# Two finest levels of the hgrn2 chunk matrix: products on VectorE and sums on GpSimd instead of 32-lane matmuls on TensorE

## The chip, the cores and the metric

The kernel runs on one core of a Trainium2 chip. The time is that of one execution of the whole program on the device, in microseconds (us). Five engines work side by side, each through its own instructions in a fixed order: TensorE (PE, matmuls; PEld, its weight loads), VectorE (DVE), ScalarE (ACT), GpSimd (POOL) and SyncE (SP, which issues the loads). They wait for each other on semaphores alone.

## The reference

Two layers work on 272 tokens (16 meta tokens and 256 others). Each layer has a mixer with three branches (retention, hgrn2, differential attention) and a convolutional feed-forward part. What the change touches is hgrn2, cut here to one chunk of 128 tokens:

```python
def step(state, xs):
    qc, kc, vc, lfc = xs                       # lfc: log of the forget gate
    cb = jnp.cumsum(lfc, axis=1)
    rel = cb[:, :, None] - cb[:, None, :]
    dec = jnp.where(causal, jnp.exp(jnp.where(causal, rel, 0.0)), 0.0)
    a = jnp.einsum('bqhd,bkhd,bqkhd->bhqk', qc, kc, dec)
    o = jnp.einsum('bhqk,bkhe->bqhe', a, vc) + jnp.einsum('bqhd,bhde->bqhe', qc * jnp.exp(cb), state)
    ...
```

The decay between a query and a key differs in each of the 128 features d, so `a` is no plain matmul. There are 8 heads of 128 features.

## The kernel before, in words

**The main stream.** Nearly all of the time goes to the dense products of the layers. Weights stand in memory as 128x128 tiles in the order of their use, eight to a chunk. A chunk is loaded (`wraw`), ScalarE makes a rounded copy (`whi`) and VectorE the rest (`wlo` = `wraw` - `whi`); three of `wraw` and four each of `whi` and `wlo` exist at a time. For each weight tile TensorE runs three matmuls over up to 272 tokens: `whi` by `xh`, `whi` by `xl`, `wlo` by `xh` (lines L900 to L902). Such a group is called a triple here. `_Weights.next` writes this.

**The order.** Nothing is issued as it is written. Every operation is recorded with an engine, an estimated cost and a due time, and `_Plan.order` sorts the whole program into one fixed order for each engine by a list schedule over these estimates. Line L592 is the recorder's, so nearly all operations but the matmuls of the main stream carry it. The main stream's place in time sets the due times of the rest (`behind`, `settle`): the work of hgrn2 is spread between triples. The estimate for a reduction over partitions is 0.4 us and 5.4 ns a column.

**hgrn2.** `hg_heads(b)` does four heads: it runs twice in a layer, so four times in the program. `k` is the tile `hf`, `q` the tile `hq`, both with features on partitions and 4 heads x 272 tokens along the free side. `total` holds the decay of each block of tokens, first the gate itself (`he`), then one level after the other in `tot`. A loop runs over the levels s = 1, 2, 4, 8, 16, 32, 64. On each level TensorE multiplies keys of left halves by queries of right halves of blocks of 2s tokens (a block of up to 32 small matmuls, tile `lev`, line L1084); VectorE puts the entries that belong to the level into `near` by a masked copy; then `q` and `k` are multiplied by `total` (two products), and the next level begins. So TensorE, in its fixed order, stands before each `lev` block until VectorE has done the two products of the level before. Level 1 also yields the diagonal. For level 2 a copy of queries (`extra`, by ScalarE) is used, and a second set of entries (right of each pair by itself) comes out of the same block. Where s is 32, `near` is copied to `at`, the matrix that `hg_outputs` multiplies by the values. The last 16 tokens go another way (`kt`, `qt`, `pm`, `am`) that the change leaves alone.

**GpSimd** normalises: `inverse` sums squares over the 128 partitions by `partition_all_reduce` (tile `hr`), for each head of each branch. It also clears tiles and copies small ones.

Of the kernel before, what the change touches and what calls it, by code (L numbers as in the profile page):

```python
# [15 lines left out]
AF = mybir.ActivationFunctionType  # L16
# [4 lines left out]
P = 128  # L21
# [3 lines left out]
T = META + SEQ  # L25
# [239 lines left out]
def _constants():  # L265
    f = np.float32
    c = np.zeros((P, C_END), f)
    c[:, C_COS_R : C_COS_R + T], c[:, C_SIN_R : C_SIN_R + T] = _rope_tables(RET_DK, 1)
    c[:, C_COS_D : C_COS_D + T], c[:, C_SIN_D : C_SIN_D + T] = _rope_tables(DA_DH, 2)
    k = np.arange(P)  # L270
    c[:, C_MASK + T - P : C_MASK + T] = np.where(k[None, :] <= k[:, None], 0.0, MASKED)
    c[:, C_IDENT : C_IDENT + P] = np.eye(P, dtype=f)
    lg = np.log1p(-np.exp2(-5.0 - np.arange(RET_HEADS, dtype=f))).astype(f)
    def decay(keys, queries):
        gap = (queries[None, :] - keys[:, None]).astype(f)
        d = np.exp(lg[None, :, None] * np.maximum(gap, 0)[:, None, :]) * f(RET_DK ** -0.5)
# [29 lines left out]
    block = [level(s, 32, 16) for s in LEVELS[2:6]] + [odd(32, 16), even(32, 32)]  # L306
    lev[:, :112] = np.tile(np.concatenate(block, axis=1), (4, 1))
# [344 lines left out]
def _trace(ctx, tc, plan, a, depth, probe):  # L652
# [26 lines left out]
    def slot(name, dt=F32):  # L679
        return new(sp, [P, 4 * T], dt, "slot", SLOTS, name)  # L680
# [13 lines left out]
    def bank(name):  # L694
        return new(bp, [P, 512], F32, "bank", 2, name)
# [4 lines left out]
    def tt(out, x, y, op):  # L700
        dve.tensor_tensor(out=out, in0=x, in1=y, op=op)
# [266 lines left out]
    for li in range(depth):  # L968
# [72 lines left out]
        def hg_heads(b):  # L1041
# [28 lines left out]
            def right(t, s):  # L1070
                return halves(t, s, t.shape[2])[:, :, :, 1, :]
# [22 lines left out]
            extra = slot("extra")  # L1094
# [3 lines left out]
            tt(right(q, 1), right(q, 1), right(total, 1), MUL)  # L1098
            room, at0 = slot("tot"), 0
            for i, s in reversed(list(enumerate(LEVELS))):  # L1100

                pl = bank("lev")
                wide = pl[:, :256].rearrange("p (g t) -> p g t", g=8)
                some = pl[:, :128].rearrange("p (g t) -> p g t", g=8)
                tokens = lambda c, t: slice(c * P + 32 * t, c * P + 32 * t + 32)
                if s == 1:
                    quarters(wide, q, lambda hd, c, t: q[:, hd, tokens(c, t)])
                    dve.copy_predicated(near, lev[:, 80:112].unsqueeze(1).to_broadcast([P, 8, 32]), wide)  # L1110
                elif s == 2:
                    act.activation(odd[:, :, :, :64].rearrange("p h c (n s) -> p h c n s", s=2),
                                   q[:, :, : 2 * P].rearrange("p h (c n two s) -> p h c n two s", c=2, two=2, s=2)[:, :, :, :, 1, :], AF.Copy)
                    quarters(wide.rearrange("p g (two t) -> p g two t", two=2), odd,
                             lambda hd, c, t: odd[:, hd, c, :].rearrange("p (two t) -> p two t", two=2)[:, :, 16 * t : 16 * t + 16])
                    fill(right(near, 2), lev[:, 48:64], wide[:, :, :16])
                    fill(right(near, 1), lev[:, 64:80], wide[:, :, 16:])
                elif s < 32:
                    quarters(some.rearrange("p g (n s) -> p g n s", s=s), q, lambda hd, c, t: right(q[:, hd : hd + 1, tokens(c, t)], s)[:, 0])
                    fill(right(near, s), lev[:, 16 * (i - 2) : 16 * (i - 1)], some)  # L1120
                elif s == 32:
                    for t in range(4):
                        here = slice(32 * t, 32 * t + 32)
                        act.activation(at[here, :, : 2 * P].rearrange("p h (c t) -> p h c t", c=2)[:, :, :, here],
                                       near[here].rearrange("p (h c) t -> p h c t", c=2), AF.Copy)

                    far = some.rearrange("p (h two) t -> p h (two t)", two=2)
                    blocks([(far[64 * n + 32 * c : 64 * n + 32 * c + 32, hd], k[:, hd, c * P + 64 * n : c * P + 64 * n + 32],
                             q[:, hd, c * P + 64 * n + 32 : c * P + 64 * n + 64]) for hd in hs for n in range(2) for c in range(2)], far, q)
                    for n in range(2):  # L1130
                        for c in range(2):
                            x = far[64 * n + 32 * c : 64 * n + 32 * c + 32]
                            to = at[64 * n : 64 * n + 32, :, c * P + 64 * n + 32 : c * P + 64 * n + 64]
                            if c:
                                act.activation(to, x, AF.Copy)
                            else:
                                dve.tensor_copy(to, x)
                else:

# [12 lines left out]
                    act.activation(at[:64, :, P + 64 : 2 * P], far[64:, :, :64], AF.Copy)  # L1152
                    act.activation(at[:, :, tail], far[:, :, 64:], AF.Copy)
# [450 lines left out]
```

## Time and profile before

| what | value |
|---|---|
| time, median of 3 runs | 1308.76 us (1308.33 to 1309.17) |
| the profiled execution's own time | 1309.57 us |
| its span in the trace | 1307.8 us |
| TensorE busy, matmuls | 1295.4 us (99%), 11774 matmuls |
| VectorE busy | 959.0 us (73%) |
| ScalarE busy | 801.6 us (61%) |
| GpSimd busy | 169.8 us (13%), 204 instructions |
| granted TensorE clock | 0.999 |

The span is the time from the first to the last instruction in the trace. Some 1.8 us of the profiled execution lie outside it, and that execution is 0.8 us above the median. An instruction's row in the timeline gives its start, its duration, engine, line, tiles (written <- read) and shape, and in brackets how long its engine had been idle and what ended that. Matmuls overlap each other, so the time that one costs TensorE is read from start to start.

### The profile page before, as it was taken

Reading aid. Unit: us, or ns where it says so; the run is one execution under the profiler, and the core shown is the slowest. Engines: PE = TensorE matmul, PEld = TensorE weight load, DVE = VectorE, ACT = ScalarE, POOL = GpSimd, SP = SyncE. Lnnn points to the kernel's source line nnn. Section 1 sums busy time; section 2 is a strip of 40 time slices with the busy share of each in tenths; the row PEclk is TensorE's granted clock in tenths of the full one; section 3 lists DMA queues with packets and bytes.
Section 4 is the critical chain, followed back from the end, with each engine's and each line's share of the span. In section 5 each row is a group of like instructions: output and inputs, shape, how many; then the busy total and the mean of one; then the engine's idle time right before and its main releaser. Section 6 shows DMA issues by size and latency. Waiting matters only on the chain.

```text
span 1307.8 us, 28691 instructions
## 1 busy us (share of the span) xinstructions
PE 1295.4 (99%) x11774; PEld 1266.6 (97%) x11774; DVE 959.0 (73%) x1589; ACT 801.6 (61%) x1332; POOL 169.8 (13%) x204
## 2 busy tenths in 40 slices
PE   9999999999999999999999999999999999999998
PEld 8999999999999999999999999999999999999986
DVE  7675787697576789886575757876986867888853
ACT  6747454746676577666456574547565775767643
POOL 5001101312222020000030011012131210200000
PEclk9999999999999999999999999999999999999999
DMA  7644543443544545555555445444445446466553
GB/s 268 202 143 160 168 160 134 146 146 129 193 131 162 179 160 176 182 175 181 177 177 186 162 152 177 150 144 146 156 147 176 142 165 202 144 199 205 200 188 112
DMA packets 60755, 219.06 MB, mean 168 GB/s; under 512 B 6864, under 2 KB 6992, under 8 KB 60624
## 3 DMA queue, kind: packets, MB, share of 16 engines
q1 hardware_dynamic: 60336, 216.71, 49.0%
q8 instruction: 92, 1.51, 0.5%
q10 hardware_dynamic: 288, 0.52, 0.1%
q14 instruction: 39, 0.32, 0.1%
HBM read 216.16 MB, written 1.05 MB: 166 GB/s over the span
## 4 chain that ended last, share of the span: by engine, by line
PE 92%; DVE 5%; ACT 1%; DMA 1%; issue 1%; SPq 0%; POOL 0%; DVEq 0%; ACTq 0%
PE main L900 27%; PE main L902 26%; PE main L901 26%; PE fo L1403 2%; PE fo L1404 2%; PE fo L1405 2%; DVE wlo L592 1%; PE lev L1084 1%; DVE two_b L592 1%; PE ds L1268 1%; PE ro L592 1%; PE ho L592 1%; PE vt L592 1%; DVE two_a L592 1%; PE do L592 1%
## 5 line engine op out<-in xcount | busy, mean ns | idle before, releaser
L900 PE MATMUL main<-xh,whi 128*128 128x272 f32 (+1 forms) x2368 | 689.7, 291 | 0.4 <-ACT whi L592 0.4
L901 PE MATMUL main<-xl,whi 128*128 128x272 f32 (+1 forms) x2368 | 672.9, 284 | 2.0 <-DVE xl L592 2.0
L902 PE MATMUL main<-xh,wlo 128*128 128x272 f32 (+1 forms) x2368 | 673.5, 284 | 1.2 <-DVE wlo L592 1.0
L592 DVE TENSOR_TENSOR wlo<-wraw,whi 128x1024 fp32r<-128x1024 f32 (+1 forms) x411 | 503.4, 1230 | 186.9 <-ACT whi L592 185.9
L592 ACT ACTIVATE whi<-wraw 128x1024 fp32r<-128x1024 f32 (+1 forms) x411 | 427.0, 1042 | 227.7 <-PE main L901 153.4
L901 PEld LDWEIGHTS main<-xl,whi 128*128 128x128 f32 x2368 | 446.1, 188 | 3.0 <-DVE xl L592 2.4
L902 PEld LDWEIGHTS main<-xh,wlo 128*128 128x128 f32 x2368 | 445.8, 188 | 2.8 <-DVE wlo L592 2.7
L900 PEld LDWEIGHTS main<-xh,whi 128*128 128x128 f32 x2368 | 446.2, 188 | 2.1 <-ACT whi L592 0.6
L592 POOL PARTITION_ALL_REDUCE hr<-hsq x36 | 72.0, 2016 | 120.9 <-ACT hsq L592 120.9
L592 DVE SCALAR_TENSOR_TENSOR two_b<-main,small,two_b 128x256 f32<-128x256 f32 (+2 forms) x144 | 65.3, 487 | 26.8 <-ACT two_b L592 25.1
L592 POOL TENSOR_TENSOR y<-h,rstd 128x272 f32<-128x272 f32 x32 | 34.6, 1113 | 317.1 <-ACT rstd L592 317.1
L592 ACT ACTIVATE two_b<-main,small 128x272 f32<-128x272 f32 (+1 forms) x72 | 37.2, 566 | 24.6 <-PE main L902 24.6
L900 PE MATMUL main<-ghi,whi 128*128 128x272 f32 x176 | 51.0, 290 | 0.0
L901 PE MATMUL main<-glo,whi 128*128 128x272 f32 x176 | 50.6, 287 | 0.0
L902 PE MATMUL main<-ghi,wlo 128*128 128x272 f32 x176 | 50.3, 286 | 0.0
L592 POOL COPY tails<-vsrc 128x32 f32<-128x32 f32 x32 | 11.8, 383 | 224.6 <-ACT vsrc L592 224.6
L900 PE MATMUL main<-b0hi,whi 128*128 128x272 f32 (+1 forms) x128 | 38.2, 298 | 0.0
L900 PE MATMUL main<-b1hi,whi 128*128 128x272 f32 (+1 forms) x128 | 37.8, 295 | 0.0
L592 ACT ACTIVATE vsrc<-main 128x544 f32<-128x544 f32 x24 | 15.0, 626 | 35.2 <-PE main L902 35.1
L900 PE MATMUL main<-yhi,whi 128*128 128x272 f32 (+1 forms) x128 | 36.4, 284 | 0.0
L901 PE MATMUL main<-b0lo,whi 128*128 128x272 f32 (+1 forms) x128 | 36.4, 284 | 0.0
L902 PE MATMUL main<-yhi,wlo 128*128 128x272 f32 (+1 forms) x128 | 36.4, 284 | 0.0
(236 smaller groups left out, 1942.3 us busy)
## 6 DMA issues: line engine op xcount, KB each, us to landing
wraw<-in_w SPq DMA_DIRECT2D x402, 512.0 KB, 3.3
h<-in_h SPq DMA_DIRECT2D x4, 272.0 KB, 5.9
dec<-in_dec SPq DMA_DIRECT2D x2, 544.0 KB, 4.9
wraw<-in_w SPq DMA_DIRECT2D x4, 256.0 KB, 5.6
const<-in_const SPq DMA_DIRECT2D x1, 937.0 KB, 6.5
gain<-in_gl SPq DMA_DIRECT2D x1, 512.0 KB, 5.1
out<-y ACTq DMA_DIRECT2D x2, 256.0 KB, 3.0
out<-y SPq DMA_DIRECT2D x2, 256.0 KB, 2.7
```

What stands on the lines that cost most here:

```text
L592: self.plan.add(self.name, lambda: f(*args, **kw), cost, outs, ins, args[2] if method == "activation" else None)
L900: nc.tensor.matmul(o, wh, hi, start=first, stop=False)
L901: nc.tensor.matmul(o, wh, lo, start=False, stop=False)
L902: nc.tensor.matmul(o, wl, hi, start=False, stop=last)
L1084: nc.tensor.matmul(o, keys, x, start=True, stop=True)
L1268: nc.tensor.matmul(ss[m][:, at : at + nk], q[half, hd, q0 : q0 + P], k[half, hd, :nk], start=True, stop=True)
L1403: nc.tensor.matmul(o, gh, wh, start=False, stop=False)
L1404: nc.tensor.matmul(o, gl, wh, start=False, stop=False)
L1405: nc.tensor.matmul(o, gh, wl, start=False, stop=end)
```

## The change

The `lev` blocks of levels 1 and 2 are taken out. In their place VectorE multiplies `q` by `k` feature by feature, and GpSimd sums the products over the 128 features with `partition_all_reduce`, 544 columns at a time; the sum stands on all partitions afterwards, so that the entry of a query can be read on its key's partition. There are five such sums in a call of `hg_heads`: one of `mine` (each odd token by itself) into the second half of `extra`, two of `prod` (each pair's left key by both its queries), and two of `prod` again on level 2 (third and fourth token of each four by the first and by the second). Masked copies, one for each 32 partitions, then bring the entries to `near`. Two slots of the tile pool more are held (`prod`, `sums`), and ScalarE's two copies into `extra` go.

```diff
-            odd = extra[:, : 8 * P].rearrange("p (h c t) -> p h c t", h=4, c=2)
+            def sums(out, prod):
+                for c in range(0, prod.shape[1], 2 * T):
+                    pool.partition_all_reduce(out[:, c : c + 2 * T], prod[:, c : c + 2 * T], P, ReduceOp.add)
...
+            extra, prod, total_of = slot("extra"), slot("prod"), slot("sums")
+            mine, own = extra[:, : 2 * T], extra[:, 2 * T :]
...
-            act.activation(odd[:, :, :, 64:], q[:, :, : 2 * P].rearrange("p h (c n two) -> p h c n two", c=2, two=2)[:, :, :, :, 1], AF.Copy)
+            tt(mine, rows(q, 2)[:, :, 1], rows(k, 2)[:, :, 1], MUL)
+            sums(own, mine)
             tt(right(q, 1), right(q, 1), right(total, 1), MUL)
+            tt(prod.rearrange("p (n s) -> p n s", s=2), rows(q, 2), rows(k, 2)[:, :, 0:1].to_broadcast([P, 2 * T, 2]), MUL)
+            sums(total_of, prod)
+            for t, here in lanes():
+                dve.copy_predicated(blocks_of[here], lev[here, 80:112]..., by_chunk(total_of, P)[here, :, :, here])
+            for t, here in lanes():
+                dve.copy_predicated(blocks_of[here]..., lev[here, 64:80]..., by_chunk(own, P // 2)[here, ...])
...
                 if s == 1:
-                    quarters(wide, q, lambda hd, c, t: q[:, hd, tokens(c, t)])
-                    dve.copy_predicated(near, lev[:, 80:112].unsqueeze(1).to_broadcast([P, 8, 32]), wide)
+                    pass
                 elif s == 2:
-                    act.activation(odd[...], q[...], AF.Copy)
-                    quarters(wide.rearrange("p g (two t) -> p g two t", two=2), odd, ...)
-                    fill(right(near, 2), lev[:, 48:64], wide[:, :, :16])
-                    fill(right(near, 1), lev[:, 64:80], wide[:, :, 16:])
+                    halves_ = [prod[:, : 2 * T], prod[:, 2 * T :]]
+                    for kk, x in enumerate(halves_):
+                        tt(x.rearrange("p (n s) -> p n s", s=2), rows(q, 4)[:, :, 2:], rows(k, 4)[:, :, kk : kk + 1].to_broadcast([P, T, 2]), MUL)
+                    sums(total_of, prod)
+                    for t, here in lanes():
+                        for kk, c in enumerate((48, 112)):
+                            dve.copy_predicated(to, mask, data)    # 32 partitions each
```

The schedule is made anew from the new list of operations, so it moves instructions. The first place is VectorE in the first call of `hg_heads` (first layer, heads 0 to 3). `wlo` rows are the main stream's weights, `extra` and `prod` the new products, `tot` the decays, `hf` and `hq` the keys and queries. Before, from the first `wlo` to the two products of level 2:

```order
L592 TENSOR_TENSOR wlo_248<-wraw_246,whi_247 128x1024
L592 TENSOR_TENSOR tot_215<-he_139 128x544
...
L592 TENSOR_TENSOR hq_36_123<-hq_36_123,he_139 128x544
L592 TENSOR_TENSOR wlo_251<-wraw_249,whi_250 128x1024
L592 TENSOR_TENSOR wlo_256<-wraw_254,whi_255 128x1024
L592 TENSOR_TENSOR hf_38_131<-hf_38_131,he_139 128x544
L592 TENSOR_TENSOR hq_36_123<-hq_36_123,he_139 128x1088
L592 COPY_PREDICATED near_213<-masks_80,lev_216 128x256
L592 TENSOR_TENSOR wlo_259<-wraw_257,whi_258 128x1024
L592 TENSOR_TENSOR hq_36_123<-hq_36_123,tot_215 128x272x2
L592 TENSOR_TENSOR hf_38_131<-hf_38_131,tot_215 128x272x2
```

The same stretch on VectorE now, from the same `wlo`; the seven rows of `tot` stand as they did and are left out at the second mark:

```order
L593 TENSOR_TENSOR wlo_248<-wraw_246,whi_247 128x1024
L593 TENSOR_TENSOR extra_214<-hq_36_123,hf_38_131 128x544
L593 TENSOR_TENSOR hq_36_123<-hq_36_123,he_139 128x544
L593 TENSOR_TENSOR prod_215<-hq_36_123,hf_38_131 128x1088
...
L593 TENSOR_TENSOR wlo_251<-wraw_249,whi_250 128x1024
L593 TENSOR_TENSOR wlo_256<-wraw_254,whi_255 128x1024
L593 TENSOR_TENSOR wlo_259<-wraw_257,whi_258 128x1024
L593 TENSOR_TENSOR prod_215<-hq_36_123,hf_38_131 128x544
...
L593 TENSOR_TENSOR wlo_281<-wraw_279,whi_280 128x1024
L593 TENSOR_TENSOR prod_215<-hq_36_123,hf_38_131 128x544
L593 TENSOR_TENSOR hf_38_131<-hf_38_131,tot_217 128x272x2
L593 TENSOR_TENSOR hq_36_123<-hq_36_123,tot_217 128x272x2
```

Four new products stand ahead of level 2's two, and one more `wlo`. The second and third writing of `prod` each stand behind a sum that reads the same half.

The second place is GpSimd at the same time. `tails` and `near` belong to the work around, `hr` is the first normalisation; a bare `ISA` row changes the set of GpSimd's programs. Before:

```order
L592 MEMSET at_209 128x1088
L592 COPY tails_195<-vsrc_196 128x32
L592 COPY tails_195<-vsrc_205 128x32
L592 MEMSET am_263 128x64
L592 MEMSET near_264 128x256
L592 ISA
L592 ISA hr_231<-hsq_230 128x272
```

Now:

```order
L593 MEMSET at_209 128x1088
L593 COPY tails_195<-vsrc_196 128x32
L593 ISA
L593 ISA extra_214<-extra_214 128x544
L593 ISA sums_216<-prod_215 128x544 x2
L593 COPY tails_195<-vsrc_205 128x32
L593 MEMSET am_263 128x64
L593 ISA sums_216<-prod_215 128x544 x2
L593 MEMSET near_264 128x256
L593 ISA hr_231<-hsq_230 128x272
```

The five sums come in one go, and the change of programs has moved from behind `near` to a place right ahead of them. In the second layer it stands behind the clearing of `at`, ahead of a copy to `tails`.

On TensorE the `lev` block of level 4, the first that is left, moves back in all four calls. Counted in triples of the main stream that stand ahead of it: from 205 to 217, from 418 to 442, from 1821 to 1831 and from 2034 to 2054. In the second and fourth call two more groups of four transposes (`vt`) now stand ahead of it.

More of the change, by code (lines that the diff above doesn't have):

```diff
@@ L305, in _constants @@
     lev = np.zeros((P, 2 * 64 + 192), f)
-    block = [level(s, 32, 16) for s in LEVELS[2:6]] + [odd(32, 16), even(32, 32)]
-    lev[:, :112] = np.tile(np.concatenate(block, axis=1), (4, 1))
+    near = level(2, 32, 16) * (np.arange(32)[:, None] % 2 == 0), level(2, 32, 16) * (np.arange(32)[:, None] % 2)
+    block = [level(s, 32, 16) for s in LEVELS[2:5]] + [near[0], odd(32, 16), even(32, 32), near[1]]
+    lev[:, :128] = np.tile(np.concatenate(block, axis=1), (4, 1))
     inner = [even(TAIL, 16), level(2, TAIL, 8), odd(TAIL, 8), level(4, TAIL, 8), level(8, TAIL, 8)]
@@ L1091, in quarters, with lanes @@
                                for hd in hs for c in range(2) for t in range(4)], out, moving)
-            extra = slot("extra")
-            odd = extra[:, : 8 * P].rearrange("p (h c t) -> p h c t", h=4, c=2)
+            def lanes():
+                return [(t, slice(32 * t, 32 * t + 32)) for t in range(4)]
+            def sums(out, prod):
+                for c in range(0, prod.shape[1], 2 * T):
+                    pool.partition_all_reduce(out[:, c : c + 2 * T], prod[:, c : c + 2 * T], P, ReduceOp.add)
@@ L1098, in hg_heads @@
+            sums(own, mine)
             tt(right(q, 1), right(q, 1), right(total, 1), MUL)
+            tt(prod.rearrange("p (n s) -> p n s", s=2), rows(q, 2), rows(k, 2)[:, :, 0:1].to_broadcast([P, 2 * T, 2]), MUL)
+            sums(total_of, prod)
+            blocks_of = near.rearrange("p (h c) t -> p h c t", c=2)
+            for t, here in lanes():
+                dve.copy_predicated(blocks_of[here], lev[here, 80:112].unsqueeze(1).unsqueeze(1).to_broadcast([32, 4, 2, 32]),
+                                    by_chunk(total_of, P)[here, :, :, here])
@@ L1099, in hg_heads @@
+            for t, here in lanes():
+                dve.copy_predicated(blocks_of[here].rearrange("p h c (n two) -> p h c n two", two=2)[:, :, :, :, 1],
+                                    lev[here, 64:80].unsqueeze(1).unsqueeze(1).to_broadcast([32, 4, 2, 16]),
+                                    by_chunk(own, P // 2)[here, :, :, 16 * t : 16 * t + 16])
             room, at0 = slot("tot"), 0
             for i, s in reversed(list(enumerate(LEVELS))):
-                pl = bank("lev")
-                wide = pl[:, :256].rearrange("p (g t) -> p g t", g=8)
@@ L1106, in hg_heads @@
-                some = pl[:, :128].rearrange("p (g t) -> p g t", g=8)
+                pl = bank("lev") if s > 2 else None
+                some = s > 2 and pl[:, :128].rearrange("p (g t) -> p g t", g=8)
                 tokens = lambda c, t: slice(c * P + 32 * t, c * P + 32 * t + 32)
                 if s == 1:
-                    quarters(wide, q, lambda hd, c, t: q[:, hd, tokens(c, t)])
-                    dve.copy_predicated(near, lev[:, 80:112].unsqueeze(1).to_broadcast([P, 8, 32]), wide)
+                    pass
```

12 lines of the change are left out of this document (8 added, 4 removed).

## The prediction

> **What bounds the kernel now.** I read the page's table of engines and chain first, then the groups of TensorE.
>
> ```profile
> PE 1295.4 (99%) x11774; PEld 1266.6 (97%) x11774; DVE 959.0 (73%) x1589; ACT 801.6 (61%) x1332; POOL 169.8 (13%) x204
> PE 92%; DVE 5%; ACT 1%; DMA 1%; issue 1%; SPq 0%; POOL 0%; DVEq 0%; ACTq 0%
> L902 PE MATMUL main<-xh,wlo 128*128 128x272 f32 (+1 forms) x2368 | 673.5, 284 | 1.2 <-DVE wlo L592 1.0
> ```
>
> TensorE is the chain for 92% of the span, and in 2368 matmuls it waited 1.0 us for `wlo`. So what is taken off TensorE counts in full, and so does each us for which it is made to stand. GpSimd's 13% is no comfort by itself: what counts is whether TensorE waits behind it.
>
> **What goes.** The timeline of TensorE shows the first `lev` block among the triples of the main stream, four transposes (`vt`), and the level 4 block of each of the four calls.
>
> ```profile
> 77.88 0.28 PE L900 MATMUL main<-xh,whi 128*128 128x272 f32 x1
> 78.25 0.29 PE L900 MATMUL main<-xh,whi 128*128 128x272 f32 x1
> 78.50 0.29 PE L902 MATMUL main<-xh,wlo 128*128 128x272 f32 x1
> 78.71 0.76 PE L1084 MATMUL lev<-hq,hf 128*32 128x32 f32 x64
> 79.64 0.28 PE L901 MATMUL main<-xl,whi 128*128 128x272 f32 x1
> 82.85 0.60 PE L592 MATMUL vt<-const,vsrc 128*128 128x128 f32 x4
> 87.96 0.74 PE L1084 MATMUL lev<-hq,hf 128*32 128x16 f32 x64
> 178.65 0.74 PE L1084 MATMUL lev<-hq,hf 128*32 128x16 f32 x64
> 744.84 0.74 PE L1084 MATMUL lev<-hq,hf 128*32 128x16 f32 x64
> 833.43 0.74 PE L1084 MATMUL lev<-hq,hf 128*32 128x16 f32 x64
> ```
>
> A triple takes 78.25 - 77.88 = 0.37 us. From L902 at 78.50 to the second matmul behind the block is 1.14 us, where two steps of the triple take 0.25. The block costs 0.89. There are eight such blocks (levels 1 and 2, four calls): 8 x 0.89 = **7.1 us off TensorE**. This is all that can be gained. ScalarE's copies into `extra` and the masked copies that read `lev` also go, but these engines are not the chain.
>
> **What comes on VectorE.** Its timeline, around the first product of each call (the answers of the four places, one after the other):
>
> ```profile
> 72.30 1.23 DVE L592 TENSOR_TENSOR wlo<-wraw,whi 128x1024 fp32r<-128x1024 f32 x1 [0.56 <-ACT whi L592]
> 73.45 0.72 DVE L592 TENSOR_TENSOR tot<-he 128x544 f32<-128x544 f32 x1
> 74.20 1.72 DVE L592 TENSOR_TENSOR tot<-tot 128x272 f32<-128x272 f32 x6
> 75.83 0.72 DVE L592 TENSOR_TENSOR hq<-hq,he 128x544 f32<-128x544 f32 x1
> 76.47 1.22 DVE L592 TENSOR_TENSOR wlo<-wraw,whi 128x1024 fp32r<-128x1024 f32 x1
> 80.50 1.28 DVE L592 TENSOR_TENSOR hq<-hq,he 128x1088 f32<-128x1088 f32 x1
> 81.71 0.45 DVE L592 COPY_PREDICATED near<-masks,lev 128x256 f32<-128x256 uint8 x1
> 90.10 0.29 DVE L592 COPY_PREDICATED near<-masks,lev 128x128 f32<-128x128 uint8 x1
> 167.85 0.72 DVE L592 TENSOR_TENSOR hq<-hq,he 128x544 f32<-128x544 f32 x1
> 168.48 0.72 DVE L592 TENSOR_TENSOR tot<-he 128x544 f32<-128x544 f32 x1
> 170.19 1.22 DVE L592 TENSOR_TENSOR wlo<-wraw,whi 128x1024 fp32r<-128x1024 f32 x1
> 730.56 0.72 DVE L592 TENSOR_TENSOR tot<-he 128x544 f32<-128x544 f32 x1
> 822.58 0.72 DVE L592 TENSOR_TENSOR hq<-hq,he 128x544 f32<-128x544 f32 x1
> ```
>
> From start to start a product of 544 columns takes 76.47 - 75.83 = 0.64 us, one of 1088 takes 1.21 (80.50 to 81.71), a `wlo` 1.15 (72.30 to 73.45), the seven rows of `tot` 2.38 (73.45 to 75.83) and their first four in the second and fourth call 1.71 (168.48 to 170.19). The masked copies now work on 32 partitions each, with as many columns as the old ones: 0.45 and 0.29.
>
> The new products ahead of level 4 are three of 544 columns and one of 1088: 3.13 us. What stood there anyway is three products of level 1 (0.64 + 0.64 + 1.21) and two of level 2 (1.28): 3.77. With `tot`, the `wlo` rows that the new order puts between, and in the second and fourth call eight masked copies (4 x 0.45 + 4 x 0.29 = 2.96), VectorE's work from the first product to the end of level 2 is, call by call:
>
> - first: 3.13 + 3.77 + 2.38 + 4 x 1.15 = 13.9 us
> - second: 3.13 + 3.77 + 1.71 + 4 x 1.15 + 2.96 = 16.2 us
> - third: 3.13 + 3.77 + 2.38 + 3 x 1.15 = 12.7 us
> - fourth: 3.13 + 3.77 + 1.71 + 3 x 1.15 + 2.96 = 15.0 us
>
> **The room for it.** TensorE comes to level 4's block at the old time, plus 0.37 us for each triple that now stands ahead of it, less the two removed blocks (1.78). In the second and fourth call two groups of four transposes more stand ahead, 0.6 us each by the row at 82.85. The first product can start where the rows above begin. First call: 87.96 + 12 x 0.37 - 1.78 - 73.45 = 17.2 us of room. Second: 178.65 + 24 x 0.37 - 1.78 + 1.2 - 167.85 = 19.1. Third: 744.84 + 10 x 0.37 - 1.78 - 730.56 = 16.2. Fourth: 833.43 + 20 x 0.37 - 1.78 + 1.2 - 822.58 = 17.7. So the work alone fits, with 3.3, 2.9, 3.5 and 2.7 us to spare. Weights are covered too: four `wlo` exist, and TensorE hardly waited for one.
>
> **What the sums do to VectorE.** Here the change fails by my reading. Rows of the two engines where a reduction meets a `wlo` (in the trace of before a reduction is of 272 columns in the first layer; that at 974.47 is of 242, that at 978.57 of 128):
>
> ```profile
> 246.64 1.89 POOL L592 PARTITION_ALL_REDUCE hr<-sum  x1 [11.16 <-DVE sum L592]
> 246.98 1.91 DVE L592 TENSOR_TENSOR wlo<-wraw,whi 128x1024 fp32r<-128x1024 f32 x1 [0.43 <-ACT whi L592]
> 974.47 1.76 POOL L592 PARTITION_ALL_REDUCE hr<-hsq  x1 [2.73 <-ACT hsq L592]
> 974.67 1.93 DVE L592 TENSOR_TENSOR wlo<-wraw,whi 128x1024 fp32r<-128x1024 f32 x1
> 233.60 1.88 POOL L592 PARTITION_ALL_REDUCE hr<-sum  x1 [6.53 <-DVE sum L592]
> 235.06 1.23 DVE L592 TENSOR_TENSOR wlo<-wraw,whi 128x1024 fp32r<-128x1024 f32 x1 [1.56 <-ACT whi L592]
> 115.14 1.23 DVE L592 TENSOR_TENSOR wlo<-wraw,whi 128x1024 fp32r<-128x1024 f32 x1 [1.59 <-ACT whi L592]
> 115.53 2.60 POOL L592 PARTITION_ALL_REDUCE hr<-hsq  x1 [14.10 <-ACT hsq L592]
> 978.57 1.08 POOL L592 PARTITION_ALL_REDUCE hr<-hsq  x1 [2.34 <-ACT hsq L592]
> ```
>
> A `wlo` that starts 0.34 us into a reduction takes 1.91 us instead of 1.22: as if it could only begin 246.98 + 0.69 - 246.64 = 1.03 us after the reduction did. At 242 columns the same working gives 974.67 + 0.71 - 974.47 = 0.91. One that starts 1.46 us in is not delayed. And a reduction that starts during a `wlo` is late by what is left of it (2.60 instead of 1.88). So the first part of a reduction and a VectorE product with two operands in the core's memory exclude each other. That part is 1.03/272 = 3.8 ns a column, and 0.91/242 the same: at 544 columns **2.06 us**. The whole reduction, by 1.88 at 272 and 1.08 at 128, is 5.6 ns a column more: 3.4 us at 544.
>
> All five reductions of a call begin before level 2's products are done: the second and third must end before `prod` may be overwritten, the fourth and fifth start as soon as it is. VectorE has products in its queue all this while. So each call adds up to 5 x 2.06 = 10.3 us: none (if a reduction fell where VectorE is idle) to 10.3 is what could fall on the path. I take 10.3, since the sums of work leave VectorE no idle time beyond the spare. TensorE then stands before level 4's block for 13.9 + 10.3 - 17.2 = 7.0, 16.2 + 10.3 - 19.1 = 7.4, 12.7 + 10.3 - 16.2 = 6.8 and 15.0 + 10.3 - 17.7 = 7.6 us: **28.8 us**. Behind TensorE's wait stands the whole main stream; nothing covers it. The later levels cost nothing more: VectorE then has only `wlo` rows and short products, and TensorE's delay gives both engines room.
>
> The Trainium skill (Advanced Engine Details and Errata, Mode Summary under VectorE Performance Modes) says that VectorE's second memory port is shared with GpSimd and that their instructions block each other. It names no part of an instruction; that reading is a rival below, since the row at 235.06 speaks for a first part only.
>
> **The change of programs.** It stands ahead of the first call's sums, behind a copy to `tails`. The trace shows no instruction for its length. Two rows bound it for the change at the program's start:
>
> ```profile
> 0.86 0.10 POOL L592 MEMSET eps<- 128x1 f32 x1
> 10.30 1.37 POOL L592 TENSOR_TENSOR sum<-sum,two_c 128x544 f32<-128x544 f32 x1 [9.34 <-ACT two_c L592]
> 74.98 0.21 POOL L592 COPY tails<-vsrc 128x32 f32<-128x32 f32 x1 [40.68 <-ACT vsrc L592]
> ```
>
> It lies between 0 and 9.3 us; the work behind it started when its data came, so nothing tells more, and I take the middle, 4.7. From the second reduction's end, 75.2 + 2 x 3.4 = 82.0 us plus the change's length, VectorE still has two writings of `prod`, `tot`, a `wlo` and level 2's products to do (2 x 0.64 + 2.38 + 1.15 + 1.28 = 6.1) and three held parts (6.2): level 4's block is free 94.3 us plus that length into the span at the earliest. The sum above has it free at 73.45 + 13.9 + 10.3 = 97.6. So the first 3.3 us cost nothing, and the rest counts in full: **1.4 us**, bounds 0 and 6.0. In the second layer the change stands right behind the clearing of `at`, long before its sums.
>
> The Trainium skill (GPSIMD Engine Reference, Instruction dispatch) gives about 6 us for loading such a program at its first call. By that price this term would be 2.7 and not 1.4, and the time 1.3 us more.
>
> **The sum.** -7.1 + 28.8 + 1.4 = +23.1 us on the profiled execution's 1309.57 us (1.8 us of them outside the span, before as after), so 1332.7; the median of the runs shown is 0.8 lower, and by it I forecast **1332 us**.
>
> **Rivals.**
>
> *The held part doesn't grow with width.* If it is 1.03 us whatever the columns, a call adds 5.2 us and TensorE waits 1.9, 2.3, 1.7 and 2.5: 8.4 us. With 1.4 and -7.1 that is +2.7, 1311.5 us. For it: the rows differ in width by little (242 to 272). Against: these two scale with width to 1%. Chance 0.18.
>
> *The wide sums hardly get in the way, and it is faster.* If VectorE loses under 0.54 us for each sum (a fifth of the least spare, 2.7 us), the work fits the room and TensorE never stands: 1308.8 - 7.1 = 1301.7 us, or up to 1.4 more with the change of programs. It needs VectorE to find gaps, for example if the sum takes its input in short bursts. For it: the plan has the room, and VectorE is idle 27% of the span. Against: the rows at 246.98 and 974.67. Chance 0.12.
>
> *The whole of a reduction blocks.* With 3.4 us each, a call adds 17 and TensorE waits 6.7 us more in each: 1359 us. Against: the row at 235.06. Chance 0.05.
>
> *The sums are slower than the line says.* If 544 columns take 5 us, GpSimd's own chain sets the end: three sums in series and level 2's products behind them, some 3 to 5 us later in each call: 1345 us. For it: reductions of 2.60 in company. Chance 0.08.
>
> That the change doesn't do what it says is out: the new order shows the eight blocks gone.
>
> **How the numbers follow.** The forecast's case has 0.57. Its own range is 1320 to 1342 (part of a held time in VectorE's idle time below; 6.0 us for the change of programs and a few waits at later levels above). With the rivals, 8 in 10 reach from 1310 to 1344. A measurement of this kernel tells 0.2%, 2.6 us, from no change. Faster has the second rival's 0.12; the same 0.06 out of the first rival; slower the rest, 0.82.
>
> **What would show it.** Right: `extra` and `sums` rows of GpSimd of about 3.4 us, 20 in all; VectorE products beside them of 2 us and more; waits of TensorE of 6 to 9 us before the first `lev` block of each call, ended by `hq` or `hf`; 512 rows of `lev` matmuls fewer (256 instructions, two rows each). Wrong: TensorE without gaps there (then the held part is short); gaps at `wlo` instead (then weights are late, and the place is another); one large gap in the first call alone (then it is the change of programs).

## The result, and the profile after

The changed kernel takes 1352.3 us (median of 5 runs, 1351.7 to 1352.5) where the kernel before, beside it on the same chip, takes 1309.1 (1308.3 to 1309.4). The ratio is 1.033 (95% interval 1.032 to 1.034): 43.2 us slower, where +23 was forecast. From the page of the changed kernel: its span, the busy time of the engines, and the chain of waits by engine.

```profile
span 1350.2 us, 27744 instructions
PE 1302.3 (96%) x11262; PEld 1272.9 (94%) x11262; DVE 1032.5 (76%) x1657; ACT 793.8 (59%) x1320; POOL 244.5 (18%) x224
PE 82%; DVE 13%; issue 2%; ACT 1%; POOL 1%; DMA 1%; SPq 0%; DVEq 0%; ACTq 0%
```

512 matmuls are gone, as they should be. VectorE's share of the chain went from 5% to 13%, but its share of the span only from 73% to 76%. That second figure hides the matter. The next view gives the busy time of each engine in four stretches of 50 us, one around each call of `hg_heads`; PEclk is the granted clock. First the kernel before, then the changed one (its later calls come later by what it has lost until then):

```profile
72.00:122.00 50.00, 50.00 (x777) 48.74 (x776) 33.45 (x56) 28.06 (x54) 6.04 (x6) 1.00 0.44 149
166.00:216.00 50.00, 50.00 (x770) 48.42 (x769) 39.69 (x71) 24.94 (x49) 1.87 (x5) 1.00 0.43 150
727.00:777.00 50.00, 50.00 (x788) 48.83 (x787) 35.86 (x59) 28.60 (x54) 4.61 (x7) 1.00 0.42 142
819.00:869.00 50.00, 50.00 (x777) 48.52 (x776) 40.38 (x74) 26.20 (x52) 3.65 (x9) 1.00 0.44 152
```

```profile
72.00:122.00 50.00, 40.26 (x514) 39.11 (x516) 43.30 (x62) 17.90 (x33) 17.93 (x9) 0.90 0.34 115
176.00:226.00 50.00, 40.90 (x509) 39.49 (x508) 49.06 (x66) 20.51 (x42) 23.41 (x12) 0.93 0.38 126
750.00:800.00 50.00, 42.34 (x575) 41.23 (x574) 47.98 (x66) 20.97 (x38) 18.86 (x10) 0.90 0.37 117
852.00:902.00 50.00, 40.59 (x513) 39.06 (x512) 49.02 (x68) 21.08 (x42) 22.39 (x12) 0.93 0.37 119
```

The third busy figure is VectorE's: 33 to 40 us of 50 before, 43 to 49 now, in three of the four calls practically all the time. The first is TensorE's: it never stood, and now it stands 9.7, 9.1, 7.7 and 9.4 us in these stretches, 35.9 together. The large waits, from TensorE's timeline (the bracket gives the idle time and what ended it):

```profile
91.19 0.48 PE L593 MATMUL vm<-const,tails 128*128 128x128 f32 x1 [4.41 <-POOL tails L593]
104.98 1.05 PE L1085 MATMUL lev<-hq,hf 128*32 128x16 f32 x64 [5.33 <-DVE hq L593]
208.28 1.06 PE L1085 MATMUL lev<-hq,hf 128*32 128x16 f32 x64 [6.77 <-DVE hf L593]
761.88 0.49 PE L593 MATMUL pm<-qt,kt 128*128 128x128 f32 x2 [2.67 <-ACT qt L593]
781.27 1.06 PE L1085 MATMUL lev<-hq,hf 128*32 128x16 f32 x64 [4.99 <-DVE hq L593]
882.07 1.05 PE L1085 MATMUL lev<-hq,hf 128*32 128x16 f32 x64 [7.19 <-DVE hf L593]
```

In calls 2 and 4 the wait stands where it was forecast, before level 4's block, near the forecast size (6.77 and 7.19; 7.4 and 7.6 were worked out). In calls 1 and 3 level 4's block comes in time, since TensorE has already stood 4.41 us before `vm` or 2.67 before `pm`, and the large wait is one level later, before level 8's block. The six large waits come to 31.4 us, where 28.8 + 1.4 = 30.2 was forecast; but only 14.0 of them stand where they were put, so that the two totals agree is luck.

After each large wait the clock is lower. The stretches behind the six waits:

```profile
91.20:94.20 3.00, 3.00 (x14) 3.00 (x15) 2.83 (x8) 1.23 (x2) 0.03 (x1) 0.52 0.00 0
105.00:111.20 6.20, 6.20 (x87) 6.16 (x88) 6.03 (x12) 1.64 (x3) 0.00 (x0) 0.50 0.52 171
208.30:213.60 5.30, 5.30 (x83) 5.26 (x84) 5.29 (x8) 1.30 (x3) 1.03 (x2) 0.51 0.56 182
761.90:766.50 4.60, 4.60 (x26) 4.60 (x27) 4.60 (x3) 2.24 (x4) 3.18 (x3) 0.63 0.13 21
781.30:787.00 5.70, 5.70 (x86) 5.66 (x87) 5.56 (x11) 1.47 (x3) 0.00 (x0) 0.50 0.58 181
882.10:886.00 3.90, 3.90 (x77) 3.86 (x78) 3.90 (x6) 0.58 (x3) 1.03 (x2) 0.50 0.46 143
```

Length times the missing share of the clock is 1.4 + 3.1 + 2.6 + 1.7 + 2.9 + 2.0 = 13.7 us. With it the books close: 35.9 standing + 13.7 at a lower clock - 7.1 removed = 42.5, and the spans differ by 42.4. The Trainium skill (TensorE: Matmul & The Clock Gate, Part 1) says that TensorE falls to half its rate after an idle window of about 3.4 us and needs one busy window to come back; these rows show the half rate, here once already behind a wait of 2.67 us.

VectorE and GpSimd in the first call, each from its timeline, show what VectorE is doing while TensorE stands:

```profile
72.96 0.72 DVE L593 TENSOR_TENSOR extra<-hq,hf 128x544 f32<-128x544 f32 x1
...
87.52 2.91 DVE L593 TENSOR_TENSOR prod<-hq,hf 128x544 f32<-128x544 f32 x1 [3.42 <-POOL sums L593]
...
95.25 0.72 DVE L593 TENSOR_TENSOR hq<-hq,tot 128x544 f32<-128x544 f32 x1
95.88 1.87 DVE L593 COPY_PREDICATED near<-masks,sums 32x256 f32<-32x256 uint8 x4
97.78 3.76 DVE L593 COPY_PREDICATED near<-masks,extra 32x128 f32<-32x128 uint8 x4
101.57 2.71 DVE L593 TENSOR_TENSOR hf<-hf,tot 128x544 f32<-128x544 f32 x1
104.21 0.71 DVE L593 TENSOR_TENSOR hq<-hq,tot 128x544 f32<-128x544 f32 x1
...
110.62 3.72 DVE L593 COPY_PREDICATED near<-masks,sums 32x128 f32<-32x128 uint8 x8
```

```profile
74.51 0.21 POOL L593 COPY tails<-vsrc 128x32 f32<-128x32 f32 x1 [40.70 <-ACT vsrc L593]
80.64 3.43 POOL L593 PARTITION_ALL_REDUCE extra<-extra  x1 [5.92 <-DVE wlo L593]
83.98 6.90 POOL L593 PARTITION_ALL_REDUCE sums<-prod  x2
90.76 0.38 POOL L593 COPY tails<-vsrc 128x32 f32<-128x32 f32 x1
...
97.92 6.82 POOL L593 PARTITION_ALL_REDUCE sums<-prod  x2 [6.69 <-DVE near L593]
```

Between level 2's `hq` (95.25) and level 4's (104.21) VectorE does eight masked copies, and the fourth and fifth sum begin only when the first four copies have read `sums`: one holds the other copies (3.76, where the four before them took 1.87), the next holds `hf` (2.71, where `hq` behind it takes 0.71). So 9 us pass before level 8's block may start. On GpSimd the copy to `tails` at 90.76, which TensorE wants for `vm`, is queued behind the change of programs and three sums.

### The profile page after: what moved, and what is told of

It is laid out like the page before. It is cut to its first block, busy times and chain, and to the rows that moved or that the text cites. A ratio compares the mean times of both kernels' runs of the same rounds, so it can differ in the third digit from the quotient of the medians.

```text
span 1350.2 us, 27744 instructions
## 1 busy us (share of the span) xinstructions
PE 1302.3 (96%) x11262; PEld 1272.9 (94%) x11262; DVE 1032.5 (76%) x1657; ACT 793.8 (59%) x1320; POOL 244.5 (18%) x224
## 4 chain that ended last, share of the span: by engine, by line
PE 82%; DVE 13%; issue 2%; ACT 1%; POOL 1%; DMA 1%; SPq 0%; DVEq 0%; ACTq 0%
PE main L901 24%; PE main L903 24%; PE main L902 24%; DVE wlo L593 2%; DVE near L593 2%; DVE hf L593 2%; PE fo L1432 1%; PE fo L1433 1%; PE fo L1434 1%; DVE hq L593 1%; PE ds L1297 1%; DVE two_b L593 1%; PE ho L593 1%; DVE prod L593 1%; PE ro L593 1%
## 5 line engine op out<-in xcount | busy, mean ns | idle before, releaser
L593 DVE TENSOR_TENSOR wlo<-wraw,whi 128x1024 fp32r<-128x1024 f32 (+1 forms) x411 | 508.8, 1245 | 171.7 <-ACT whi L593 170.1
L901 PEld LDWEIGHTS main<-xh,whi 128*128 128x128 f32 x2368 | 451.1, 191 | 1.3 <-ACT whi L593 0.2
L593 POOL PARTITION_ALL_REDUCE sums<-prod x16 | 59.3, 3744 | 28.7 <-DVE near L593 24.4
L1085 PEld LDWEIGHTS lev<-hq,hf 128*32 128x32 f32 x1088 | 13.5, 121 | 27.3 <-issue 14.3
L1085 PE MATMUL lev<-hq,hf 128*32 128x16 f32 (+2 forms) x1088 | 15.5, 198 | 24.3 <-DVE hf L593 14.0
```

The lines of the kernel that those rows point to most:

```text
L593: self.plan.add(self.name, lambda: f(*args, **kw), cost, outs, ins, args[2] if method == "activation" else None)
L901: nc.tensor.matmul(o, wh, hi, start=first, stop=False)
L1085: nc.tensor.matmul(o, keys, x, start=True, stop=True)
```

## The experiments

### What each part costs

**Without the sums.** The order of all engines stays that of the changed kernel.

```diff
-                    pool.partition_all_reduce(out[:, c : c + 2 * T], prod[:, c : c + 2 * T], P, ReduceOp.add)
+                    part = out[:, c : c + 2 * T]
+                    plan.add("pool", lambda part=part: nc.gpsimd.memset(part, 0.0), 0.4 + 5.4e-3 * 2 * T, [part], [prod[...]])
```

> Leaves out the 20 sums: each is a clearing of the same 544 columns by GpSimd, which the planner counts like the sum, so the order of all engines is that of the changed kernel. Theory (the loss comes from the sums alone: parts of them that hold VectorE, and work that waits for them on GpSimd): TensorE waits nowhere by more than 1 us before a lev block, the 7.1 us off TensorE show, and the time is 1300 to 1305. Rival (VectorE's added products and masked copies don't fit the room): waits of 3 us or more before the first or second lev block of a call stay, and the time is 1315 to 1335.

Measured: 1312.1 us, ratio 1.0023 (1.0013 to 1.0034), between the two ranges. The long waits are gone and the clock stays full, so most of the loss does come with the sums. But the theory's bound of 1 us doesn't hold, and the 7.1 us don't show: behind level 4's block TensorE waits once in each call, 1.90, 1.70, 1.14 and 1.10 us, for `near`, the tile that the masked copies write. The first two of these waits:

```profile
103.81 0.74 PE L1085 MATMUL lev<-hq,hf 128*32 128x16 f32 x64 [1.90 <-DVE near L593]
195.80 0.41 PE L593 MATMUL vt<-const,vsrc 128*128 128x128 f32 x2 [1.70 <-DVE near L593]
```

**Products only.** Sums replaced as above, and the masked copies counted by the planner but not issued.

```diff
-                dve.copy_predicated(blocks_of[here], ...)
+                plan.add("dve", lambda: None, <its cost>, [out], [mask, data])     # all 16
```

> Leaves out the sums (clearings in their place, as in the run without sums) and the 16 masked copies, so VectorE has only the four new products, 3.1 us a call, in the order of the changed kernel. Theory (they lie within VectorE's slack): the whole 7.1 us show, 1300 to 1304. Rival (even the products, or the order made for the sums, cost TensorE waits): 1306 to 1312.

Measured: 1302.1 us, ratio 0.9947 (0.9932 to 0.9962). The removed blocks are worth 7.0 us, as worked out (7.1), and the four products cost nothing that shows. The 10.0 us between this run and the one without sums are the masked copies. (The clearings, 0.55 us each, slow VectorE a little too: an `hf` by a scalar took 1.73 us beside the first of call 2, and 1.25 at that place in the kernel before. What follows is counted from a base that has them in it.)

**No copies, but the sums.** The masked copies are again counted by the planner but not issued.

> Leaves out the 16 masked copies of each call that bring the sums to near (64 of 32 partitions); the planner still counts them, so the order is that of the changed kernel. Theory by now (VectorE is full in these stretches; a call loses what VectorE gets on top of a slack of some 9 us, wherever the wait shows): VectorE is spared 9.4 us a call, a call's loss falls from 12.4 to about 3, and the time is 1310 to 1322. Rival (the sums' own chain on GpSimd and the held parts set the pace, and the copies lie in VectorE's waits for them): 1338 to 1350.

Measured: 1334.7 us, ratio 1.0196 (1.0181 to 1.0211): between the two expectations and nearer the rival. The copies are worth 17.6 us of the 43.2, not 30.

**The sums alone**, added to the kernel before:

```diff
             extra = slot("extra")
+            spare = slot("sums")
+            for c in (2, 0, 2, 0, 2):
+                pool.partition_all_reduce(spare[:, c * T : (c + 2) * T], const[:, c * T : (c + 2) * T], P, ReduceOp.add)
```

> The kernel before with 20 more reductions of 544 columns, five in each call, of a constant into a spare tile: nothing waits for them and no VectorE work is added. Theory (held parts come to some 7 to 10 us of VectorE a call, about its slack): 1309 to 1316. Rival (the held parts alone make most of the 43 us): 1325 to 1345.

Measured: 1339.9 us, ratio 1.024 (1.022 to 1.026). The rival's number came: 20 sums for which nothing waits cost 30.8 us. (The new order starts two of the five of calls 1 and 3 some 35 and 42 us ahead of the other three.) The engines' line of its page, and the second call's sums with VectorE beside them and TensorE's wait (three answers of the timeline):

```profile
PE 1304.1 (97%) x11774; PEld 1274.7 (95%) x11774; DVE 1000.3 (75%) x1589; ACT 803.2 (60%) x1332; POOL 239.5 (18%) x224
```

```profile
172.31 17.36 POOL L592 PARTITION_ALL_REDUCE sums<-const  x5
```

```profile
174.80 0.35 DVE L592 TENSOR_SCALAR hf<-hf,keep 128x272 f32<-128x272 f32 x1
...
175.93 2.47 DVE L592 TENSOR_SCALAR hf<-hf,keep 128x272 f32<-128x272 f32 x1
178.33 4.54 DVE L592 TENSOR_TENSOR wlo<-wraw,whi 128x1024 fp32r<-128x1024 f32 x2
182.79 2.97 DVE L592 TENSOR_TENSOR hq<-hq,he 128x544 f32<-128x544 f32 x1
```

```profile
185.91 1.08 PE L1084 MATMUL lev<-hq,hf 128*32 128x32 f32 x64 [4.50 <-DVE hq L592]
```

VectorE's busy time grew by 1000.3 - 959.0 = 41.3 us for 20 sums, a held operation counting as busy: 2.07 us a sum. That is the held part of the prediction (2.06); held time that fell where VectorE had nothing to do would not be in this figure. `hq`, 0.72 us of work, takes 2.97 here, and level 1's block waits for it.

The six numbers together (medians in us; VectorE's busy time from the pages):

| kernel | time | against before | VectorE busy |
|---|---|---|---|
| before | 1309.1 | | 959.0 |
| products only | 1302.1 | -7.0 | 969.7 |
| products and copies | 1312.1 | +2.9 | 995.4 |
| products and sums | 1334.7 | +25.5 | 1005.7 |
| products, copies and sums | 1352.3 | +43.2 | 1032.5 |
| before, and the sums alone | 1339.9 | +30.8 | 1000.3 |

From the products' 1302.1 on, copies cost 10.0, sums 32.6, both together 50.2: 7.6 more than the two apart. A likely reason, which no run tests by itself, is that both fill the same idle time of VectorE.

**Level 1 alone** the new way; level 2 stays a `lev` block, by the lines that serve levels 4 to 16.

```diff
-                elif s == 2:
-                    halves_ = ...            # products, sums and copies of level 2
-                pl = bank("lev") if s > 2 else None
+                pl = bank("lev") if s > 1 else None
```

> Level 1 alone goes the new way (three sums, two products, eight masked copies a call); level 2 stays a lev block of 16 columns on TensorE, whose 0.9 us a call come back. Theory (VectorE gets 1.85 + 3.8 + 3 held parts of 2.06 = 11.8 us a call on a slack of 9; 4 x 2.8 lost, 3.6 gained): 1312 to 1322. Rival (level 2's series of sum, product and sum makes the loss, and level 1 alone has none): 1304 to 1308.

Measured: 1336.1 us, ratio 1.021 (1.019 to 1.022), far above both expectations. Three sums and eight copies a call bring the greater part of the loss; VectorE's busy time is 1003.2. In this order at least, the slack of 9 us on which the expectation rested isn't there.

### Is it the place, or VectorE as a whole?

**Tiles of their own for level 2**, so that no sum waits for a copy and no product for a sum:

```diff
                 elif s == 2:
+                    prod, total_of = slot("prod2"), slot("sums2")
```

> Level 2 gets tiles of its own for its products and its sums, so its products wait for no sum of level 1, and the fourth and fifth sum wait for no masked copy. The planner puts the lev blocks 3 to 14 triples earlier. Theory (held parts of VectorE and its work add up; the order of waiting only decides before which block TensorE stands): waits of 5 to 9 us in each call stay, before level 4's block instead of level 8's in calls 1 and 3, and the time is 1340 to 1356. Rival (the loss is the chain of reuse: sum, product, sum, copy, sum): the waits fall under 3 us and the time is 1312 to 1328.

Measured: 1355.3 us, ratio 1.035 (1.034 to 1.037). The time is the theory's, so the chain of reuse isn't the cause; the place is not quite. The waits stand before both blocks: in call 1 the one before level 8's shrank to 3.64, and 0.90 came before level 4's; in call 4 there are 5.00 and 2.42 where there was one of 7.19. TensorE's idle time, span less busy, is 51.8 us by its page (1354.8 - 1303.0), and 47.9 in the changed kernel.

**Later blocks.** A delay in the planner alone:

```diff
+                    plan.ops[-1].lag = {(0, 8): 6.0, (1, 4): 8.0}.get((b, s), 0.0)     # added to the op's ready time
```

> The changed kernel with a delay in the planner alone: 6 us ahead of level 8's block in calls 1 and 3 and 8 us ahead of level 4's in calls 2 and 4, which puts these blocks 17, 20, 17 and 21 triples later in TensorE's order. No operation is added or taken. Theory (the loss is TensorE standing before these four blocks, 24.3 us, and the half clock behind it, 10.5): both go, and the time is 1312 to 1324. Rival (VectorE falls behind by as much elsewhere, at wlo or at later levels): 1335 to 1352.

Measured: 1351.4 us, ratio 1.032 (1.031 to 1.034): the rival. TensorE doesn't wait for these four blocks any more, but at the same time for something else:

```profile
106.46 0.69 PE L594 MATMUL pm<-qt,kt 128*128 128x64 f32 x2 [5.17 <-ACT qt L594]
...
210.84 0.60 PE L904 MATMUL main<-xh,wlo 128*128 128x272 f32 x1 [5.32 <-DVE wlo L594]
...
781.98 0.69 PE L594 MATMUL pm<-qt,kt 128*128 128x64 f32 x2 [5.03 <-ACT qt L594]
...
883.56 0.59 PE L904 MATMUL main<-xh,wlo 128*128 128x272 f32 x1 [6.68 <-DVE wlo L594]
```

These rows end their waits 0.7 to 2.6 us after the old ones (104.98, 208.28, 781.27, 882.07). In calls 2 and 4 it is now the main stream's own weights that are late. VectorE works through one queue; as long as that queue's order makes all its results late, it helps little that TensorE asks for another one first.

**The clock.** Idle matmuls in the four waits:

```diff
+                    for _ in range(idle):                  # 24 ahead of these four blocks
+                        nc.tensor.matmul(spare[:, :P], ones_d, ones_d, start=True, stop=True)
                     for o, keys, x in calls:
```

> The changed kernel in the same order, with 24 idle matmuls (ones by ones, 128x128, about 0.22 us each, 5.2 us together) on TensorE right ahead of the four lev blocks at which it waited longest (5.33, 6.77, 4.99 and 7.19 us). They have nothing to do with the result. Theory (a wait of some us costs TensorE half its clock for up to 6.8 us behind it, 13.7 us in all, 10.5 of them behind these four waits): with TensorE at work in the waits the clock stays at 1.0, and the time falls by 5 to 11 us, to 1341 to 1347. Rival (the lower clock in the records costs nothing, since VectorE sets the pace behind the waits anyway): 1351 to 1355.

Measured: 1354.0 us, ratio 1.034 (1.033 to 1.036): the rival again. The mean clock rose from 0.986 to 0.994, but TensorE only came sooner to the next wait, and VectorE did its work when it always did. Behind the filled waits stand new ones of 1.72, 1.84, 1.63 and 1.21 us, one in each call, all ended by `near`. Two answers of the timeline, TensorE's with the first of them, and VectorE's:

```profile
114.76 0.74 PE L1087 MATMUL lev<-hq,hf 128*32 128x16 f32 x64 [1.72 <-DVE near L593]
```

```profile
104.26 0.71 DVE L593 TENSOR_TENSOR hq<-hq,tot 128x544 f32<-128x544 f32 x1
...
110.68 3.70 DVE L593 COPY_PREDICATED near<-masks,sums 32x128 f32<-32x128 uint8 x8
```

In the changed kernel VectorE's two rows start at 104.21 and 110.62. So the half clock is in the books there, but full speed behind these four waits would not have been worth its 3.1 + 2.6 + 2.9 + 2.0 = 10.6 us. The waits before `vm` and `pm` were not filled.

**The same with the sums alone**, where VectorE has less to do behind the wait:

```diff
+                    quarters(wide, q, ..., idle=25, spare=pl)      # ahead of level 1's block
```

> The kernel with the 20 reductions alone, plus 25 idle matmuls (5.4 us) right ahead of level 1's block of each call, where it waited 5.46, 4.50, 5.37 and 4.50 us and then ran 17.6 us at half the clock. Theory (the half clock behind a wait costs its 8.5 us, where VectorE is not behind afterwards): with the waits filled 1331 to 1336. Rival (VectorE sets the pace behind the waits too, so the clock costs nothing): 1339 to 1344.

Measured: 1336.8 us, ratio 1.021 (1.019 to 1.023): 3.2 less than without the idle matmuls, just outside what the theory gave and clear of the rival. The first of the four groups of idle matmuls, with the block behind it, in TensorE's timeline (a matmul has two rows):

```profile
79.79 5.74 PE L1084 MATMUL lev<-ones_d 128*128 128x128 f32 x50
85.47 0.76 PE L1086 MATMUL lev<-hq,hf 128*32 128x32 f32 x64
```

They take 85.47 - 79.79 = 5.68 us in each call, 22.7 together, where TensorE had stood 19.8. The granted clock is 0.999 in this run. That more work gave less time is the clock: 3.2 + 2.9 = some 6 of the 8.5 us.

### Can a better order hide it?

**A planner that knows the held part.**

```diff
+                    t = start(op, max(t0, engines["dve"]) if op.held else t0)
...
+            if op.held:                                  # a reduction: 3.9 ns a column
+                engines["dve"] = max(engines["dve"], t + op.held)
```

> The changed kernel with one thing more in the planner: a reduction starts only when VectorE is free and then takes VectorE away for 3.9 ns a column (2.1 us at 544). Nothing is added or taken; level 8's block moves from triple 242 to 282 in call 1, and VectorE's weights stand ahead of other work. Theory (the loss is VectorE's queue, planned without the held parts, being late for TensorE): most of it goes, 1308 to 1325; what stays is the masked copies, which the planner counts at 0.20 to 0.34 us and the trace at 0.47. Rival (VectorE simply has too much to do in these stretches, in any order): 1338 to 1352.

Measured: 1330.2 us, ratio 1.016 (1.014 to 1.017). The order alone gives back 22 us, more than half, but less than expected.

**And the copies at 0.47 us.**

> As the run whose planner knows the held parts, and the planner counts a masked copy on 32 partitions at 0.47 us as the trace has it. Theory: 1306 to 1320, and 2 to 8 us under the run whose planner knows the held parts alone. Rival (VectorE has too much to do in any order): 1338 to 1352.

Measured: 1327.2 us, ratio 1.014 (1.013 to 1.016). That is 3.0 us less, within the 2 to 8 expected, and the time is again above the expectation. The two longest waits that are left are for other results of VectorE, here a `dq`, which reads a result of the main stream, and a `wlo`:

```profile
207.63 0.56 PE L909 MATMUL main<-xh,whi 128*128 128x272 f32 x1 [3.88 <-DVE dq L599]
...
842.73 0.39 PE L911 MATMUL main<-xh,wlo 128*128 128x272 f32 x1 [2.82 <-DVE wlo L599]
```

**That planner, and no copies at all.**

> As the run whose planner knows the held parts, with the 16 masked copies of each call left out of program and plan: what that order would reach if the copies cost nothing. Theory (held parts and copies together are VectorE's excess; planned for, the held parts alone leave waits of about 1 us a call and the 7.1 us off TensorE show in part): 1304 to 1314, so no version with sums on GpSimd gets under the kernel before by more than about 5 us. Rival (the held parts cannot be hidden in any order): 1318 to 1328.

Measured: 1315.3 us, ratio 1.0044 (1.0028 to 1.0061), 1.3 us above the theory's range. Even with no copies at all and an order made for the held parts, the kernel before is faster; no version run here that has the sums beats it. Copies of full width, which would need masks of 128 columns, were not tried.

## Why the prediction was wrong

**Right: what is removed.** 7.1 us forecast, 7.0 measured with the products only.

**Right: the held part.** 2.06 us a sum forecast, 2.07 in the run with the sums alone. A sum of 544 columns takes 3.43 (3.4 forecast), so the rival with sums of 5 us falls. The rival in which the whole reduction blocks came nearest in time (1359), but not by its mechanism: 20 x 3.4 would have made VectorE 68 us busier, not 41.3. A held part of 1.03 us whatever the width would have made it 21, and sums that hardly get in the way none; so these two rivals fall as well. The Trainium skill (SBUF — State Buffer) has the port that the two engines share held for the whole instruction; the measurement decides for a part of it.

**Right in length, wrong in place: the change of programs.** The first sum starts 80.64 - 74.72 = 5.92 us after the copy ahead of it, and its input had been ready since 73.7: 5.9 us, 4.7 taken. The price of about 6 us from the Trainium skill (GPSIMD Engine Reference, Instruction dispatch) was the better one. Its effect was put in the wrong place: not level 4's block but the copy to `tails`, queued behind change and sums, made TensorE wait (4.41, for `vm`). The new order, shown ahead of the prediction, has this copy behind the sums, and the prediction did not ask who waits for it. No run took this wait away by itself, so how much of the 4.41 is the change and how much the sums stays open.

**Wrong: "The later levels cost nothing more: VectorE then has only `wlo` rows and short products."** This is the step that failed. In the changed kernel itself TensorE waits 5.33 and 4.99 us at a later level, before level 8's block of calls 1 and 3, and the work that VectorE has there is masked copies and products that a sum holds. The runs price it. The prediction counted eight masked copies in each of two calls, 2 x 2.96 = 5.9 us of its 28.8, and none behind level 4's block; measured beside the sums, the copies are worth 17.6. Products, sums and change of programs stood in it with 28.8 - 5.9 + 1.4 = 24.3; measured without the copies they are 1334.7 - 1302.1 = 32.6. So the copies lack 11.7 and the rest 8.3, together 20.0 of the 20.1 us (43.2 - 23.1) by which the forecast fell short. The 8.3 were not taken apart further. There are 64 copies, and two groups of rows, of the kernel without sums, give their time when no sum holds them:

```profile
L593 DVE COPY_PREDICATED near<-masks,sums 32x128 f32<-32x128 uint8 (+1 forms) x48 | 21.3, 443 | 1.0
L593 DVE COPY_PREDICATED near<-masks,extra 32x128 f32<-32x128 uint8 x16 | 7.1, 444 | 0.4
```

28.4 us of VectorE. The old 0.29 us for 128 columns did not carry over to 32 partitions: the new copies take 0.44 with 128 columns as with 256, and there are four for each old one.

**Wrong: the room.** It was taken up to level 4's block alone; for what comes behind it the prediction only says that TensorE's delay gives both engines room. In the stretches of a call VectorE had 10 to 17 us of 50 idle, and the change gives it (1032.5 - 959.0) / 4 = 18.4 more per call. The idle time stands in the first windows above, which are of the kernel before. The order matters too: with a planner that knows the held parts, 22 of the 43.2 us come back with the same work.

**Left out: the clock.** The forecast put nothing on it, without a reason. In the books of the trace most of what is missing stands here: 13.7 us at a lower clock and 35.9 - 30.2 = 5.7 of standing. But idle matmuls gained nothing in the changed kernel, where VectorE is late behind the waits too, and some 6 of 8.5 us with the sums alone, where it has less to do there. So I read the clock here as the form in which VectorE's lateness shows, and it isn't added to the copies' 17.6.

**Wrong: when the fourth and fifth sum start.** The prediction has them start as soon as `prod` is overwritten, and overlooked that they overwrite `sums`, which the copies still read; hence the wait before level 8's block in calls 1 and 3. The run with tiles of their own shows that this moved waits and cost nothing by itself.

## What to carry to other kernels

Work that leaves the engine on the chain is only a gain if the engine that takes it is idle in that stretch: read the windows around the change, and set the whole added time of each engine against the idle time there, to the end of the stretch and not to the first consumer. A reduction on GpSimd costs VectorE too: put its held part into the planner like work of VectorE's own. Cut into pieces of 32 partitions, a masked copy cost 0.44 us a piece here, about what the whole one of 256 columns took (0.45).

## What the hardware showed

- A sum over 128 partitions of fp32 held VectorE back for about 3.8 ns a column (2.07 us at 544 columns), also in work with one tensor operand: in the run with the sums alone an `hf` by a scalar took 2.47 us (175.93), and 0.35 where it started 2.5 us into a sum (174.80, the sum at 172.31). The Trainium skill (GPSIMD Engine Reference, Specifications) names instructions in a two-port mode beside those with two inputs; the row fits that, but no run here shows in which mode VectorE worked. The masked copies are held as well: in the changed kernel one of the 16 from `extra` took 2370 ns, where the median is 440:

```profile
L593 DVE COPY_PREDICATED near<-masks,extra x16: 433/440/2370, 97.8 to 877.2; 32x128 f32<-32x128 uint8 x16
```

- In the changed kernel the lower clock came after waits of 2.67 us and more. Reckoned at half speed it lasted 4.6 x 0.37 / 0.5 = 3.4 us behind the wait of 2.67, and 6.8 around the end of the wait at 781.27: 5.7 behind it and 5.0 x 0.11 / 0.5 = 1.1 within it, where the granted clock was 0.89 (776.3 to 781.3). In the kernel without sums a wait of 1.90 us brought none (0.999 in the mean).
